# Where a hybrid decoder trunk prepares its weights: low halves moved from GpSimd to VectorE, high halves all on ScalarE, weights loaded in 512 KB pieces

## The chip, the cores and the metric

The kernel runs on one core of one Trainium2 chip. That core has TensorE (PE in the profile, its weight loads PEld), VectorE (DVE), ScalarE (ACT), GpSimd (POOL) and SyncE (SP, which here only issues transfers). Each engine works through its own list of instructions strictly in order. The metric is the device time of one launch in microseconds (us), as the median of several runs.

## The reference, cut to what matters

Four layers, with the token mixers A, B, C, A. Each layer applies a normed mixer and a normed gated feed-forward block, all in float32, on 256 tokens of 1024 features.

```
for i in range(DEPTH):
    y = rms_norm(h, g[0])
    y = dilated_attention(...) | sink_window_attention(...) | nsa_attention(...)
    h = h + rms_norm(y, g[1])
    y = conv_ffn(rms_norm(h, g[2]), w_up, conv_w, conv_b, w_down)
    h = h + rms_norm(y, g[3])
```

A has 16 heads in three dilated groups (its input weights are 1024 x 9216), B has sliding windows with a learned sink logit per head, C has compressed, selected and windowed keys, where the compression is a small product of its own (`w1`, `w2`). The feed-forward block is 1024 to 2 x 2816 and back. All weights together are some 240 MB, each read once.

## The kernel before, in words

**Split numbers.** TensorE multiplies in a format with fewer bits than float32. So every operand is kept as a high and a low half, `src = hi + lo`, and each product is three matmuls: high by high, high by low, low by high (`mm3`, lines 308 to 310). For activations and weights alike, `split` (lines 267 to 273) makes `hi` by a rounding copy (line 272 on ScalarE, or line 270 on VectorE) and `lo` by a subtraction (line 273, on VectorE or GpSimd).

**Weights.** They are packed on the host into units of 128 x 1024 float32 (512 KB), in the order in which they are used. `U` units make one tile `raw`, loaded by one transfer that SyncE issues (`load`, line 277); here `U = 2`, so a tile has 1 MB, and the tag has two buffers. `next_unit` takes the next unit and splits it into `wh` and `wl`, which have six buffers each (`WBUFS`); a few units of each output product lie in a pool of their own. A `raw` buffer is free for the next load when the last subtraction that reads it is done. A `wh`/`wl` buffer is free when TensorE's last matmul with it is done.

**Who splits a unit.** `pool_every` = n sends the low half of every n-th unit to GpSimd; 0 sends none. `vhi` = n sends the high half of every n-th unit to VectorE. Both are set stage by stage from the table `TUNED` on line 47:

```
gp = self.pool_every and u % self.pool_every == 0
vh = self.vhi and u % self.vhi == 0
self.split(hi, lo, self.raw[:, j * UNIT : (j + 1) * UNIT], nc.gpsimd if gp else None, vh)
```

Before the change the entries are: `AEV` 3 and `AQ` 3 (A's heads: every third low half on GpSimd), `AO` 2 (A's output weights: every second), `EVB1` 1 (B from its keys and values on: every one), `EVB4` 1 with `VHB` 1 (B's output weights: low half on GpSimd, high half on VectorE), `EVC4` 1 with `VHC` 3 (C's output weights: low half on GpSimd, every third high half on VectorE), `EVF` 6 (the feed-forward's up product: every sixth low half on GpSimd).

**Stages.** In each of the four layers: a mixer, then the feed-forward block. A mixer begins with `early` (four units, token tile 0 while the norm of tile 1 still runs, then tile 1 once `yT`, the transposed and split input, is there), goes on with the other projections, then works pair of heads by pair of heads: logits `s` (line 815), minimum and exponential (line 489 on VectorE, line 490 on ScalarE), division (line 499 on VectorE, and lines 924 in B and 1123 in C on GpSimd), transposition `pT`, split into `pt`, product `ot` (line 531), `o`, `oT`, and the product `y_o` with the output weights. B needs `nsink`, the negated sinks, 128 x 16 (line 875, on VectorE), for its first minimum. C compresses its keys first (products `hid`), makes `kc` (line 999) and eight copies `vc` of the compressed values (line 1003, all on VectorE), and its logits `lc` on the compressed keys need `kc`. The feed-forward's up product has 22 blocks of two units each, every block followed by a convolution and a gated activation (lines 1165 to 1173, and the split of `act`) on VectorE and ScalarE; the down product has 22 units.

**Order.** A scheduling layer records the program and writes out each engine's list. It decides the order on each engine from its own estimates, so an edit can move instructions that it does not name.

Of the kernel before, what the change touches and what calls it, by code (L numbers as in the profile page):

```python
# [19 lines left out]
P = 128  # L20
D = 1024
# [14 lines left out]
ROW_B, ROW_C, NROW = 1024, 1408, 1792  # a head's biases by distance: A's groups 2, 1 and 0 in 256, 256 and 512, B's and C's in 384  # L36
SCALE = 0.125
UNIT = 1024
U = 2
# [7 lines left out]
TUNED = {'DUPM': 'pool', 'EVC2': '0', 'EVC3': '0', 'CS': 'gg', 'CM': '13', 'BM': '13', 'FREE': '0', 'EVB1': '1', 'EVB4': '1', 'EVC1': '0', 'EVC4': '1', 'EVF': '6', 'BS': 'gv', 'AS': 'vv', 'AEV': '3', 'TAIL': '2', 'CH1': '1', 'CR4': '0', 'CR6': '0', 'BR4': '0', 'BR6': '1', 'XF': '3', 'XA': '2', 'XB': '3', 'XC': '2', 'PFH': '1', 'WARM': '0', 'RG': 'V', 'ORD': '1', 'E1': '3', 'G1': '1', 'X1': '1', 'GATE': 'G', 'CH0': '0', 'CW0': '9', 'CW1': '9', 'PB': '6', 'PTB': '3', 'VHB': '1', 'VHC': '3', 'BPO': '4', 'CPO': '4', 'BLAG': '1', 'CLAG': '1', 'FDB': 'v', 'FDC': 'v', 'FD': 'v', 'FDL': 'v', 'QB': '5', 'VB': '3', 'PA': '6', 'BA': '2', 'AO': '2', 'AQ': '3', 'AV': '0'}  # L47
# [24 lines left out]
# ---------------------------------------------------------------- layout  # L72
def unit_cols(w, cols):
    """w-stationary: 128 columns of w as [p, k block, column]."""
    return w[:, cols].reshape(KB, P, -1).transpose(1, 0, 2).reshape(P, -1)


def tok_units(w):
    """tokens-stationary: 512 columns of w as four units of [p, 2 k blocks, 512]."""
    blocks = w.reshape(KB, P, 512).transpose(1, 0, 2)  # L80
    return [blocks[:, 2 * i : 2 * i + 2].reshape(P, -1) for i in range(4)]


def a_units(w_in, w_o):
    """Mixer A's columns: (group, q/k/v, head, dim)."""
# [27 lines left out]
def pair_cols(r):  # L113
    """Columns of heads r and 8 + r."""
    return np.concatenate([np.arange(r * HD, (r + 1) * HD), np.arange((8 + r) * HD, (9 + r) * HD)])
# [11 lines left out]
def c_units(w_in, w1, w_o):  # L127
    HQ = H * HD
    kv = [slice(HQ + i * P, HQ + (i + 1) * P) for i in range(6)]  # k_c v_c k_s v_s k_w v_w
# [46 lines left out]
def pack_conv(conv_w, conv_b):  # L176
    """[layer, p, (block, gate/val), tap 0..2 and the bias]"""
    both = np.concatenate([conv_w, conv_b[:, None]], 1)  # layer, 4, 2 * D_FF
    return both.reshape(DEPTH, 4, 2, NFF, P).transpose(0, 4, 3, 2, 1).reshape(DEPTH, P, NFF * 8)
# [12 lines left out]
def shape_constants():  # L192
    """Buckets by distance (times 1 / SCALE) for the rows of biases, masks of mixer C."""
    rows = []  # distances and which of them count
# [22 lines left out]
def halves(first, end):  # L217
    """(block, half): block by block, the last two half by half"""
# [4 lines left out]
# ---------------------------------------------------------------- device  # L223
class Trunk:
# [20 lines left out]
    # PSUM: one tile of two banks, six of one  # L245
# [21 lines left out]
    def split(self, hi, lo, src, engine=None, vh=False):  # L267
        """src = hi + lo exactly, each with 12 significant bits."""
# [6 lines left out]
    def load(self, c):  # L275
        raw = self.wpool.tile([P, U * UNIT], F32, tag="raw", bufs=2, name=f"raw{c}")
        self.nc.sync.dma_start(raw, self.ins["weights"][c])
        return raw
# [24 lines left out]
    def mm3(self, out, lhs, rhs, start, stop):  # L303
        """(lh + ll)(rh + rl) without ll * rl."""
# [7 lines left out]
    # ------------------------------------------------------------ setup  # L312
    def setup(self):
# [8 lines left out]
        self.ahead = [self.load(0)]  # L322
        if int(TUNED.get("X1", "1")):
            self.ahead.append(self.load(1))
            nc.sync.dma_start(self.h[1], ins["x"][P:])
        else:
            nc.sync.dma_start(self.h[1], ins["x"][P:])
            self.ahead.append(self.load(1))
# [6 lines left out]
    def bias_setup(self):  # L335
        """Rows of -8 * (bias or mask) by distance, per head and mask, to DRAM."""
# [18 lines left out]
    def toeplitz(self, dst, head, first, *dims):  # L355
        """dst[p, x] = row[first + p + x]; dims: others than these"""
# [5 lines left out]
    # ------------------------------------------------------------ norms  # L362
    def rstd(self, ms, name):
        """(sum of the two halves' mean squares + eps) ** -0.5"""
# [14 lines left out]
    def square(self, ms, i, x, name):  # L379
        """ms[i] = sum(x ** 2) / D"""  # L380
# [3 lines left out]
    def post_norm(self, t, y, g, name):  # L384
        """h += rms_norm(y) * g"""
# [29 lines left out]
    def transpose_in(self, t, z, yT, name):  # L415
        """yT[:, k, t * 128 ...] = z block k, transposed and split."""
# [17 lines left out]
    # ------------------------------------------------------------ products  # L434
    def proj(self, out, yT, unit):
        """out[n, tok] += w unit (128 columns) by y."""
# [4 lines left out]
    def proj_tok(self, toks, out, yT, units, nk=4):  # L441
        """out[tok, n] for 128 tokens: units hold nk k blocks of n columns each."""
# [7 lines left out]
    def early(self, yT, outs, late):  # L450
        """Columns of tok_units, [n, tok] into outs (four [128, 256]); `late` makes the second token tile of yT."""
# [18 lines left out]
    def rows_mm(self, y, xT, unit, half, start, stop):  # L470
        """Half of y[tok, 1024] += x block by 128 rows of w."""
# [3 lines left out]
    # ------------------------------------------------------------ attention pieces  # L475
# [5 lines left out]
    def stats(self, n, name):  # L481
        """Columns for -max and the sums of n softmaxes."""
        return [self.small.tile([P, n], F32, tag=f"{w}{n}", bufs=6, name=f"{w}_{name}") for w in ("nm", "den")]

    def exps(self, p, s, bias, st, c, floor=BIG):
        """p = exp(logit - max), logit = SCALE * s + bias; floor: minus one more logit, or more than any."""
# [16 lines left out]
    def p_transposed(self, parts, name):  # L503
        """The parts' transposes side by side: [:, 0] high, [:, 1] low."""
# [9 lines left out]
    def pv(self, out, v, parts, name, start, stop):  # L514
        """out[:, 0] + out[:, 1] (by p high and low), or out[:, 0] if padded, += [vh | vl]' p; parts: k0 q0, k0 q1, k1 q1"""
# [17 lines left out]
    def fold(self, o, a, ps, name, how):  # L533
        """o[64 a ...] = (vh p_hi + vl p_hi) + vh p_lo"""
# [49 lines left out]
    def out_proj(self, name, more, gains=False):  # L584
        """Products with w_o: a function of token tile, pair and half."""
# [18 lines left out]
    def out_done(self, part, y, done, finish):  # L604
        """The products with w_o from pair `done` on, token tile 0 first."""
# [14 lines left out]
    def stacked(self, ps):  # L620
        """For the heads a of a pair: [:, a, 0] has q high in the head's rows and q low in the other's,
        [:, a, 1] has k high in both, [:, a, 2] k low in the head's rows and zeros."""
# [13 lines left out]
    # ------------------------------------------------------------ mixers  # L636
    def mixer_a(self, yT, L, finish, late):
# [12 lines left out]
        def proj_v(jobs, late=None, then=None):  # L650
            """Values of group g, pairs hp and hp + 1; the tokens of groups 1 and 2 in turns, for all keys of a token
            have its parity."""
# [20 lines left out]
        def attend_s(hp):  # L673
            """Token tile t: tokens 2 p + t. Key tiles: 0, 1 of group 0, then the queries' own of groups 1 and 2."""
# [110 lines left out]
    def proj_pair(self, yT, r, q):  # L785
        """q of pairs r and r + 1"""
# [5 lines left out]
    def q_done(self, q, r, ps):  # L792
        """q[:, r, a]: high in the rows of head a of pair r, low in the other's."""
# [6 lines left out]
    def k_done(self, kd, kl, ps):  # L800
        """kd[:, i, a]: k_i high of head a in both halves; kl[:, i, a]: k_i low in the rows of head a, else zeros."""
# [19 lines left out]
    def ps_s(self, one, name):  # L821
        """Two banks for logits."""
# [8 lines left out]
    def pairs(self, yT, q, attend_s, attend_pv, L, finish, hook=None):  # L831
        """Attention of all pairs, products with w_o behind it; q of the first four pairs is there."""
# [34 lines left out]
    def mixer_b(self, yT, L, finish, late):  # L867
# [7 lines left out]
        nc.vector.tensor_scalar(nsink, sink, -1.0, None, op0=ALU.mult)  # L875
# [16 lines left out]
        v = att.tile([P, 4, P], F32R, name="v")  # (key tile, group), [vh | vl]  # L892
# [48 lines left out]
    def compress(self, att, ps, L, kc, vc, slot):  # L941
        """Compressed keys (columns by group; high in both halves, low in the group's) and values (a copy per slot of 16 rows)."""
# [62 lines left out]
    def mixer_c(self, yT, L, finish, late):  # L1005
# [19 lines left out]
        # selected and window keys and values, gates; the attention's tiles lie below those of the compression  # L1025
# [287 lines left out]
```

## Time and profile before

| | |
|---|---|
| timed runs (us) | 1626.03, 1627.21, 1627.77; median 1627.21 |
| the profiled execution | span 1624.6 us from the first to the last instruction |
| busy, share of the span | PE 95%, DVE 76%, ACT 60%, POOL 23% |
| TensorE's mean granted clock | 0.985 of full speed |
| weights | 237 loads of 1024 KB, 4.9 us from issue to landing (median) |
| low halves `wl` | 376 on VectorE, 97 on GpSimd |
| high halves `wh` | 463 on ScalarE, 10 on VectorE |

Of the profiled execution only its span is shown; it stands 2.6 us under the median of the timed runs, which also hold what lies around the span. How to read the page and its views: busy time is time in which the engine executes, including an instruction that has started and is held up inside. In the timeline each row gives start, duration, engine, line, operation, what is written from what, how many in a row were merged, and in brackets how long the engine had been idle before and what ended that. PEclk 1.00 is TensorE's upper level of 2.4 GHz, 0.50 its lower one of 1.2 GHz.

### The profile page before, as it was taken

The numbers are of one execution on the slowest core, as the hardware profiler recorded it, in microseconds if no ns is written. First come the engines' busy times: TensorE is split into PE (matmuls) and PEld (weight loads), VectorE is DVE, ScalarE is ACT, GpSimd is POOL, SyncE is SP. The second block draws the span as 40 slices with busy tenths as digits, with TensorE's granted clock in tenths as the row PEclk, the third lists the DMA queues.
The fourth block names the chain that finished last, engine by engine and source line by source line (L and its number), as shares of the span: only waits on it lengthen the run. The fifth ranks groups of instructions, "written<-read, shape, count | busy, mean of one in ns | idle before, by whom it ended". The sixth has DMA issues, their size and how long they took to land. (4 is left out here: it accounts for less than half of the span.)

```text
span 1624.6 us, 28567 instructions
## 1 busy us (share of the span) xinstructions
PE 1541.3 (95%) x10968; PEld 1429.8 (88%) x10968; DVE 1235.0 (76%) x2154; ACT 973.1 (60%) x1715; POOL 366.2 (23%) x334
## 2 busy tenths in 40 slices
PE   7999999999997799999985999999999999999998
PEld 6999998799986679998884879998999999889986
DVE  5778897698755978985588869975687879669864
ACT  5566665576544566664465857654566667557642
POOL 1443323111004611100125401100342432211100
PEclk9999999999999899999997999999999999999999
DMA  6655556455454526555562035546465556455543
GB/s 231 208 191 180 188 177 204 135 205 183 158 206 141 169 75 202 200 184 206 172 214 92 20 132 201 192 153 233 164 205 183 190 172 195 142 180 203 202 174 112
DMA packets 69737, 283.21 MB, mean 174 GB/s; under 512 B 7152, under 2 KB 36336, under 8 KB 39264
## 3 DMA queue, kind: packets, MB, share of 16 engines
q1 hardware_dynamic: 67392, 273.37, 50.1%
q0 software_dynamic: 2208, 8.01, 1.4%
q8 instruction: 87, 1.43, 0.4%
q14 instruction: 50, 0.41, 0.1%
HBM read 280.19 MB, written 1.16 MB: 173 GB/s over the span
## 5 line engine op out<-in xcount | busy, mean ns | idle before, releaser
L272 ACT ACTIVATE wh<-raw 128x1024 fp32r<-128x1024 f32 x463 | 480.4, 1056 | 354.5 <-DMA raw<-in_weights_dram 150.8
L273 DVE TENSOR_TENSOR wl<-raw,wh 128x1024 fp32r<-128x1024 f32 x376 | 474.7, 1277 | 169.9 <-ACT wh L272 167.4
L308 PE MATMUL up<-yT,wh 128*128 128x256 f32 x1280 | 359.6, 281 | 4.5 <-ACT wh L272 2.3
L273 POOL TENSOR_TENSOR wl<-raw,wh 128x1024 fp32r<-128x1024 f32 x97 | 235.0, 2428 | 557.1 <-ACT wh L272 495.8
L309 PE MATMUL up<-yT,wh 128*128 128x256 f32 x1280 | 359.1, 281 | 0.0
L310 PE MATMUL up<-yT,wl 128*128 128x256 f32 x1280 | 359.0, 281 | 0.0
L308 PEld LDWEIGHTS up<-yT,wh 128*128 128x128 f32 x1280 | 242.8, 190 | 5.2 <-ACT wh L272 2.5
L310 PEld LDWEIGHTS up<-yT,wl 128*128 128x128 f32 x1280 | 242.6, 190 | 0.0
L309 PEld LDWEIGHTS up<-yT,wh 128*128 128x128 f32 x1280 | 240.3, 188 | 0.2
L309 PE MATMUL qk<-yT,wh 128*128 128x256 f32 x768 | 215.0, 280 | 0.0
L308 PE MATMUL qk<-yT,wh 128*128 128x256 f32 x768 | 214.9, 280 | 0.0
L310 PE MATMUL qk<-yT,wl 128*128 128x256 f32 x768 | 214.9, 280 | 0.0
L1168 DVE SCALAR_TENSOR_TENSOR c<-up,cw,c 128x255 f32<-128x255 f32 (+1 forms) x352 | 164.2, 477 | 15.4 <-ACT c L1165 12.6
L310 PEld LDWEIGHTS qk<-yT,wl 128*128 128x128 f32 x768 | 144.9, 189 | 2.1 <-issue 1.5
L309 PEld LDWEIGHTS qk<-yT,wh 128*128 128x128 f32 x768 | 145.1, 189 | 1.5 <-issue 0.7
L308 PEld LDWEIGHTS qk<-yT,wh 128*128 128x128 f32 x768 | 145.1, 189 | 1.5 <-ACT vt L272 0.7
L309 PE MATMUL y_ff<-wl,act 128*128 128x512 f32 x352 | 138.6, 394 | 0.0
L310 PE MATMUL y_ff<-wh,act 128*128 128x512 f32 x352 | 138.3, 393 | 0.0
L308 PE MATMUL y_ff<-wh,act 128*128 128x512 f32 x352 | 135.2, 395 | 0.0
L308 PE MATMUL v<-wh,yT 128*128 128x256 f32 x400 | 114.0, 286 | 1.9 <-ACT wh L272 1.6
L1165 ACT ACTIVATE c<-up,cw 128x256 f32<-128x256 f32 x176 | 96.7, 552 | 31.8 <-DVE c L1168 31.5
L309 PE MATMUL v<-wl,yT 128*128 128x256 f32 x400 | 113.7, 285 | 0.7 <-DVE wl L273 0.7
(218 smaller groups left out, 2942.4 us busy)
## 6 DMA issues: line engine op xcount, KB each, us to landing
raw<-in_weights_dram SPq DMA_DIRECT2D x237, 1024.0 KB, 4.9
bias<-rows SPq DMA_DIRECT2D x160, 128.0 KB, 3.7
gain<-in_norm_gains_dram POOLq DMA_DIRECT2D x15, 512.0 KB, 5.1
out_dram<-h SPq DMA_DIRECT2D x2, 512.0 KB, 2.6
h<-in_x_dram SPq DMA_DIRECT2D x2, 256.0 KB, 3.0
gain<-in_norm_gains_dram SPq DMA_DIRECT2D x1, 512.0 KB, 6.4
h<-in_x_dram SPq DMA_DIRECT2D x1, 512.0 KB, 12.3
onehot<-in_onehot_dram SPq DMA_DIRECT2D x1, 448.0 KB, 12.8
```

What stands on the lines that cost most here:

```text
L272: self.nc.scalar.activation(hi, src, AF.Copy)
L273: (engine or self.nc.vector).tensor_tensor(lo, src, hi.bitcast(F32), op=ALU.subtract)
L308: mm(out, lh, rh, start=start, stop=False)
L309: mm(out, lh, rl, start=False, stop=False)
L310: return mm(out, ll, rh, start=False, stop=stop)
L1165: nc.scalar.activation(c[:, j], u, AF.Identity, bias=w[3], scale=w[2])
L1168: nc.vector.scalar_tensor_tensor(c[:, j, n:], in0=u[:, : S - n], scalar=w[k], in1=c[:, j, n:], op0=ALU.mult, op1=ALU.add)
```

## The change

1. `U` is 1 in place of 2 and the tag `raw` has four buffers in place of two: 473 loads of 512 KB in place of 237 of 1 MB, in the same 2 MB of buffers. The start loads four such tiles ahead in place of two large ones.
2. `EVB1`, `EVB4`, `EVC4`, `EVF` and `AO` become 0: outside A's heads every low half of a weight is made on VectorE. GpSimd keeps the 40 of A's heads.
3. `VHB` and `VHC` become 0: every high half is made on ScalarE.
4. `nsink` is made on ScalarE.

Comments and docstrings are taken out as well, which changes no instruction.

```diff
-U = 2
+U = 1
...
-        raw = self.wpool.tile([P, U * UNIT], F32, tag="raw", bufs=2, name=f"raw{c}")
+        raw = self.wpool.tile([P, U * UNIT], F32, tag="raw", bufs=4, name=f"raw{c}")
         self.nc.sync.dma_start(raw, self.ins["weights"][c])
...
-        self.ahead = [self.load(0)]
+        self.ahead = [self.load(0), self.load(1)]
         if int(TUNED.get("X1", "1")):
-            self.ahead.append(self.load(1))
+            self.ahead += [self.load(2), self.load(3)]
             nc.sync.dma_start(self.h[1], ins["x"][P:])
...
-        nc.vector.tensor_scalar(nsink, sink, -1.0, None, op0=ALU.mult)
+        nc.scalar.activation(nsink, sink, AF.Copy, scale=-1.0)
```

In the table `TUNED`: `EVB1`, `EVB4`, `EVC4`, `VHB` from 1 to 0, `VHC` from 3 to 0, `EVF` from 6 to 0, `AO` from 2 to 0; the other entries stay.

**VectorE at the entry of B**, from the norm's second token tile to the first minimum. Before (`yT` is the input of the products, `q`, `kl` and `vT` come out of B's projections, `L489` is the first minimum):

```order
L426 TENSOR_TENSOR yT_1_0_5589<-zT_0_1_0_5771,yT_1_0_5588 128x4x128
L875 TENSOR_SCALAR nsink<-sink 128x16
L426 TENSOR_TENSOR yT_1_0_5589<-zT_0_1_1_5778,yT_1_0_5588 128x4x128
L798 TENSOR_TENSOR q<-q_0_5717,q 64x2x256
L798 TENSOR_TENSOR q<-q_1_5718,q 64x2x256
L798 TENSOR_TENSOR q<-q_0_5717,q 64x2x256
L798 TENSOR_TENSOR q<-q_1_5718,q 64x2x256
L809 TENSOR_TENSOR kl<-kv_5827,kd 64x256 x2
L888 COPY vT<-kv_5827 128x256
L489 ISA p_1_0_0_5910,nm_0_5904<-s_0_0_5906,bias_0_0_5908,nsink 128x128
```

Now:

```order
L426 TENSOR_TENSOR yT_1_0_5735<-zT_0_1_0_5921,yT_1_0_5734 128x4x128
L426 TENSOR_TENSOR yT_1_0_5735<-zT_0_1_1_5928,yT_1_0_5734 128x4x128
L273 TENSOR_TENSOR wl_5981<-raw_5978,wh_5980 128x1024
L273 TENSOR_TENSOR wl_6011<-raw_6008,wh_6010 128x1024
L273 TENSOR_TENSOR wl_6097<-raw_6094,wh_6096 128x1024
L273 TENSOR_TENSOR wl_6127<-raw_6124,wh_6126 128x1024
L273 TENSOR_TENSOR wl_6199<-raw_6196,wh_6198 128x1024
L273 TENSOR_TENSOR wl_6229<-raw_6226,wh_6228 128x1024
L798 TENSOR_TENSOR q<-q_0_5863,q 64x2x256
L798 TENSOR_TENSOR q<-q_1_5864,q 64x2x256
L273 TENSOR_TENSOR wl_6470<-raw_6467,wh_6469 128x1024
L273 TENSOR_TENSOR wl_6476<-raw_6473,wh_6475 128x1024
```

`nsink` no longer stands between the two halves of `yT`, and eight of B's fourteen low halves stand on VectorE before its `q` are finished.

**VectorE in C**, from the compressed keys `kc` and values `vc` to the logits of the next pair. Before:

```order
L798 TENSOR_TENSOR q<-q_9446,q 64x2x256
L999 TENSOR_TENSOR kc_8811<-cmp_9333,kc_8810 64x16
L273 TENSOR_TENSOR vhl<-cmp_9336,vhl 128x64
L1003 TENSOR_SCALAR vc<-vhl,cst 128x128 x6
L999 TENSOR_TENSOR kc_8811<-cmp_9333,kc_8810 64x16
L1003 TENSOR_SCALAR vc<-vhl,cst 128x128 x2
L798 TENSOR_TENSOR q<-q_9446,q 64x2x256
L489 ISA p_2_1_0_9574,nm_1_0_9576<-s_1_0_0_9578,bias_1_0_9572 128x128
```

Now:

```order
L999 TENSOR_TENSOR kc_9041<-cmp_9581,kc_9040 64x16
L1111 RECIPROCAL den_0_1_9633<-den_0_1_9633 128x4
L273 TENSOR_TENSOR vhl<-cmp_9584,vhl 128x64
L999 TENSOR_TENSOR kc_9041<-cmp_9581,kc_9040 64x16
L1117 TENSOR_TENSOR rg_0_1_9649<-den_0_1_9633,gate 128x4
L1003 TENSOR_SCALAR vc<-vhl,cst 128x128 x8
L273 TENSOR_TENSOR wl_10260<-raw_10257,wh_10259 128x1024
L798 TENSOR_TENSOR q<-q_9694,q 64x2x256
L273 TENSOR_TENSOR wl_10278<-raw_10275,wh_10277 128x1024
L273 TENSOR_TENSOR wl_10266<-raw_10263,wh_10265 128x1024
L798 TENSOR_TENSOR q<-q_9694,q 64x2x256
L273 TENSOR_TENSOR wl_10284<-raw_10281,wh_10283 128x1024
```

Both parts of `kc` now come ahead of all eight `vc`, and four low halves of the output weights have taken the place behind them; the other four stand a little earlier or later in the same list.

## Rows read from the trace of the kernel before

**Rows 1.** The page, part 1: busy us, share of the span, instructions

```profile
PE 1541.3 (95%) x10968; PEld 1429.8 (88%) x10968; DVE 1235.0 (76%) x2154; ACT 973.1 (60%) x1715; POOL 366.2 (23%) x334
```

**Rows 2.** Windows: length; PE, PEld, DVE, ACT, POOL busy; PEclk; DMA share; GB/s

```profile
320.00:425.00 105.00, 102.70 (x874) 102.53 (x873) 93.45 (x150) 72.38 (x119) 14.38 (x6) 1.00 0.56 192
...
512.00:516.00 4.00, 4.00 (x10) 3.19 (x11) 0.00 (x0) 0.00 (x0) 0.00 (x0) 0.53 0.82 281
520.00:587.00 67.00, 54.16 (x347) 47.32 (x346) 59.50 (x166) 43.65 (x130) 31.23 (x26) 0.92 0.35 103
835.00:880.00 45.00, 27.74 (x185) 23.46 (x184) 37.94 (x74) 25.19 (x62) 26.19 (x16) 0.82 0.49 165
```

**Rows 3.** Groups by line: operation, shapes, count | busy us, mean ns | idle before

```profile
L272 ACT ACTIVATE wh<-raw 128x1024 fp32r<-128x1024 f32 x463 | 480.4, 1056 | 354.5 <-DMA raw<-in_weights_dram 150.8 <-PE up L309 70.7 <-PE qk L309 51.9
L273 DVE TENSOR_TENSOR wl<-raw,wh 128x1024 fp32r<-128x1024 f32 x376 | 474.7, 1277 | 169.9 <-ACT wh L272 167.4 <-issue 1.0
...
L273 POOL TENSOR_TENSOR wl<-raw,wh 128x1024 fp32r<-128x1024 f32 x97 | 235.0, 2428 | 557.1 <-ACT wh L272 495.8 <-PE up L310 26.2 <-PE s L815 17.3
```

**Rows 4.** Timeline at the entry of B, 502 to 513 us: VectorE, GpSimd, TensorE

```profile
502.39 9.54 DVE L875 TENSOR_SCALAR nsink<-sink 128x16 f32<-128x16 f32 x1 [1.21 <-DMA sink<-in_b_sinks_dram]
...
502.61 9.28 POOL L273 TENSOR_TENSOR wl<-raw,wh 128x1024 fp32r<-128x1024 f32 x4
...
512.00 0.80 PE L310 MATMUL early<-wh,yT 128*128 128x512 f32 x1 [7.74 <-DVE yT L426]
```

**Rows 5.** Inside B, 520 to 590 us: VectorE's timeline and groups; TensorE's waits

```profile
541.18 0.15 DVE L915 TENSOR_TENSOR e<-nm,sink 128x4 f32<-128x4 f32 x1
...
L270 DVE CAST wh<-raw 128x1024 fp32r<-128x1024 f32 x8 | 6.7, 874 | 0.0
...
L917 DVE TENSOR_TENSOR den<-den,e 128x4 f32<-128x4 f32 x8 | 5.2, 647 | 0.0
...
PE ot L531 <- DVE pt L273: 5.2, 2, 4.7
...
PE s L815 <- DVE nm L489: 3.8, 2, 3.3
```

**Rows 6.** Inside C, 835 to 880 us: VectorE's and GpSimd's timeline, TensorE's waits

```profile
850.08 10.17 DVE L1003 TENSOR_SCALAR vc<-vhl,cst 128x128 fp32r<-128x128 f32 x6
...
850.71 9.26 POOL L273 TENSOR_TENSOR wl<-raw,wh 128x1024 fp32r<-128x1024 f32 x4
...
PE lc L1060 <- DVE kc L999: 8.5, 1, 8.5
...
PE ot L531 <- DVE pt L273: 4.0, 1, 4.0
```

**Rows 7.** Feed-forward, up product, 339 to 343 us: GpSimd and VectorE

```profile
339.47 2.40 POOL L273 TENSOR_TENSOR wl<-raw,wh 128x1024 fp32r<-128x1024 f32 x1 [12.81 <-ACT wh L272]
...
339.73 2.42 DVE L273 TENSOR_TENSOR act<-g,act 128x256 fp32r<-128x256 f32 x1 [0.30 <-ACT act L272]
...
342.47 0.41 DVE L273 TENSOR_TENSOR act<-g,act 128x256 fp32r<-128x256 f32 x1
```

**Rows 8.** Entry of the feed-forward block: loads; TensorE's waits in layers 0 and 1

```profile
314.48 13.65 SPq L277 DMA_DIRECT2D raw<-in_weights_dram  x4
...
PE up L308 <- ACT wh L272: 2.3, 1, 2.3
...
PE up L308 <- DVE c L1168: 1.8, 1, 1.8
```

**Rows 9.** The page, part 6, DMA issues: count, KB each, median us to landing

```profile
raw<-in_weights_dram SPq DMA_DIRECT2D x237, 1024.0 KB, 4.9
...
gain<-in_norm_gains_dram POOLq DMA_DIRECT2D x15, 512.0 KB, 5.1
```

**Rows 10.** TensorE's timeline at the kernel's start and in C's compression

```profile
12.55 0.58 PE L308 MATMUL v<-wh,yT 128*128 128x256 f32 x1 [1.63 <-ACT wh L272]
...
828.07 0.44 PE L1043 MATMUL gt<-ident,gT 128*128 128x128 f32 x2 [3.29 <-ACT gT L1040]
```

More of the change, by code (lines that the diff above doesn't have):

```diff
@@ L46 @@
 WBUFS = 6
-TUNED = {'DUPM': 'pool', 'EVC2': '0', 'EVC3': '0', 'CS': 'gg', 'CM': '13', 'BM': '13', 'FREE': '0', 'EVB1': '1', 'EVB4': '1', 'EVC1': '0', 'EVC4': '1', 'EVF': '6', 'BS': 'gv', 'AS': 'vv', 'AEV': '3', 'TAIL': '2', 'CH1': '1', 'CR4': '0', 'CR6': '0', 'BR4': '0', 'BR6': '1', 'XF': '3', 'XA': '2', 'XB': '3', 'XC': '2', 'PFH': '1', 'WARM': '0', 'RG': 'V', 'ORD': '1', 'E1': '3', 'G1': '1', 'X1': '1', 'GATE': 'G', 'CH0': '0', 'CW0': '9', 'CW1': '9', 'PB': '6', 'PTB': '3', 'VHB': '1', 'VHC': '3', 'BPO': '4', 'CPO': '4', 'BLAG': '1', 'CLAG': '1', 'FDB': 'v', 'FDC': 'v', 'FD': 'v', 'FDL': 'v', 'QB': '5', 'VB': '3', 'PA': '6', 'BA': '2', 'AO': '2', 'AQ': '3', 'AV': '0'}
+TUNED = {'DUPM': 'pool', 'EVC2': '0', 'EVC3': '0', 'CS': 'gg', 'CM': '13', 'BM': '13', 'FREE': '0', 'EVB1': '0', 'EVB4': '0', 'EVC1': '0', 'EVC4': '0', 'EVF': '0', 'BS': 'gv', 'AS': 'vv', 'AEV': '3', 'TAIL': '2', 'CH1': '1', 'CR4': '0', 'CR6': '0', 'BR4': '0', 'BR6': '1', 'XF': '3', 'XA': '2', 'XB': '3', 'XC': '2', 'PFH': '1', 'WARM': '0', 'RG': 'V', 'ORD': '1', 'E1': '3', 'G1': '1', 'X1': '1', 'GATE': 'G', 'CH0': '0', 'CW0': '9', 'CW1': '9', 'PB': '6', 'PTB': '3', 'VHB': '0', 'VHC': '0', 'BPO': '4', 'CPO': '4', 'BLAG': '1', 'CLAG': '1', 'FDB': 'v', 'FDC': 'v', 'FD': 'v', 'FDL': 'v', 'QB': '5', 'VB': '3', 'PA': '6', 'BA': '2', 'AO': '0', 'AQ': '3', 'AV': '0'}
 XF = int(TUNED.get("XF", "3"))
@@ L327, in setup @@
             nc.sync.dma_start(self.h[1], ins["x"][P:])
-            self.ahead.append(self.load(1))
+            self.ahead += [self.load(2), self.load(3)]
         self.ident = self.const.tile([P, P], F32, name="ident")
```

## The prediction, as it was put on record

> **What bounds the kernel now.** The page's first part comes first: TensorE is busy for 1541.3 of the 1624.6 us [rows 1]. So nothing can be won where TensorE works without a pause, and the question is what the change does to the 83 us in which it does not, and to the stretches in which it runs at its lower clock. The windows say where these are: in the feed-forward's up product TensorE is busy for 102.7 of 105 us at full clock, but in B for 54.2 of 67 us and in C, between 835 and 880 us, for 27.7 of 45 us at 0.82 of full speed [rows 2]. In B and C VectorE is the busiest engine of the window (59.5 and 37.9 us), and GpSimd is busy for 31.2 and 26.2 us [rows 2], mostly with low halves of weights at 2.4 us each [rows 3].
>
> The timelines then show what VectorE is busy with. At B's entry `nsink`, an instruction on 128 x 16 numbers, lasts 9.54 us, and ends when four back-to-back low halves on GpSimd end (502.61 + 9.28 = 511.89 us). The second half of `yT` stands behind it, and TensorE sits idle for 7.74 us until it comes [rows 4]. In C six small copies `vc` last 10.17 us in all, beside four GpSimd low halves of 9.26 us; `kc` stands behind them, and TensorE waits 8.5 us for it [rows 6]. In the up product a split of `act` takes 2.42 us beside a GpSimd low half and 0.41 us without one [rows 7]. I read this as: while GpSimd works on a weight, those VectorE instructions cannot proceed. The low halves that GpSimd takes over therefore do not relieve VectorE; each blocks it for up to 2 us and saves it 1.28 us [rows 3].
>
> **The change part by part.** All terms are changes of the end time.
>
> *B's entry.* No low half runs on GpSimd there any more, and `nsink` has left VectorE's list. The 7.74 us go. When TensorE resumed, it ran at 0.53 of full speed for the 4 us of the window behind [rows 2], with a matmul of 0.80 us [rows 4]; without the pause I expect full speed, which saves 4.0 x 0.47 = 1.9 us. What comes in: eight low halves, 8 x 1.28 = 10.2 us [rows 3], ahead of or among the `q`. They lie beside TensorE's rest of `early` and B's key product, and `q` waits for those anyway; if that cover were 3 to 4 us short, the term would be 6. Take -9.6, ends -6 and -9.6.
>
> *Inside B.* VectorE loses eight high halves (6.7 us) and the stalls: eight small sums L917 at 0.647 us mean, against 0.15 us for an instruction of the same size, are 4.0 us [rows 5]. It gains the six other low halves, 7.7 us. Net -3 us on the busiest engine, more if the stalls of instructions not listed go too. TensorE's waits on VectorE in this stretch are 5.2 + 3.8 = 9.0 us [rows 5]: that is the most that can come back. ScalarE takes eight high halves more, 8.4 us on 43.7 of 67 [rows 2, 3], and does not become the bound. Take -4, ends 0 and -9.
>
> *C's entry into attention.* The wait of 8.5 us for `kc` [rows 6] goes: `kc` now precedes `vc`, and nothing on GpSimd holds either. Take -8.5, lower end -6 if the added low halves push `kc` back.
>
> *Inside C.* VectorE gets eight low halves, 10.2 us, and loses two high halves and the small stalls. It has 45 - 37.9 = 7 us idle in the window [rows 2]. One more wait of TensorE is on VectorE, 4.0 us for `pt` [rows 6]. Take -3, ends 0 and -4.
>
> *Up product of the feed-forward.* In a window of 105 us GpSimd makes six low halves [rows 2]. VectorE takes them, 6 x 1.28 = 7.7 us, and is rid of up to six stalls of 2 us. Even with no stall gone it would be at 93.5 + 7.7 = 101.2 of 105 us, and TensorE has no gap of weight in this stretch. Take 0, upper end +2 over all four blocks.
>
> *A's output weights.* Four low halves per layer go to VectorE, 5.1 us each time, at the end of A's attention. GpSimd's instructions leave the same stretch. Take 0, ends -2 and +4.
>
> *Loads of 512 KB.* SyncE issues 237 more transfers, off the path. What matters is the turn of a buffer: a tile of 1 MB becomes free only after two low halves, and its successor lands 4.9 us after its issue [rows 9]. At the feed-forward's entry the first free tile is issued at 314.48 us, and TensorE then waits 2.3 us for a high half in layer 0, and 1.8 us in layer 1 behind the same train [rows 8]. With units freed one by one the first load starts about one low half earlier, and half the bytes land no later. Take -3 of these 4.1 us, ends 0 and -4.1. In C's compression, where units are used fastest, TensorE waits 3.29 us for `gT` [rows 10], which stands on ScalarE among high halves that wait for loads: take -2, ends 0 and -3.3. At the start the first matmul waits 1.63 us for the first high half [rows 10], and a tile of half the size lands sooner: take -1.5, ends 0 and -1.6.
>
> The nearest row for a 512 KB load is the gain vector's, 5.1 us [rows 9]. It is issued from GpSimd and reads one row 128 times, so I take it as the upper end; the lower is half of 4.9 us, and with four loads in flight either will do, since the up product uses a unit in 105 / 874 x 24 = 2.9 us [rows 2] and a buffer thus has 4 x 2.9 = 11.5 us to turn. The Trainium skill (DMA: Bandwidth & Descriptors, section Bandwidth) speaks against this edit: transfers should be batched to at least 1 MiB for 75% of peak, and from its 0.95 us for 64 KB and 6.15 us for 1 MB an estimate for 512 KB is 3.4 us, about a tenth more per byte. By the rule the three load terms would be nil and the sum smaller by 6.5 us; no run here shows a 512 KB weight load yet.
>
> *Sum:* -9.6 - 4 - 8.5 - 3 - 3 - 2 - 1.5 = -31.6 us on the profiled span of 1624.6, so 1593.0. The median of the timed runs is 2.6 us above that span, so I say **1595.6 us**. The low ends of all terms together give about -6 to -12, the high ends about -42.
>
> **The rivals.**
> *VectorE becomes the bound of B and C.* The big waits go, but the added low halves (14 and 8 of them, 28 us in all) fill the room, TensorE waits elsewhere for `pt` and `nm`, and the inner terms and the load terms vanish: -18 us or less, 1605 to 1614 us. For it: VectorE is at 89% in B's window. Against it: much of that is stall.
> *The stall has another cause.* If `vc` and `yT` were slow for a reason of their own, neither wait goes, VectorE just gets more work, and only the load terms stay: 1621 to 1628 us. Against it: the stalled spans end with GpSimd's instructions, three times at different stages.
> *Half-size loads become the bound (slower).* In the four up products a unit is due every 2.9 us, and four buffers allow 11.5 us from issue until the low half is done. Conversion takes 1.06 + 1.28 us and its queueing a few us; the point is a landing time of about 8 us. At 9.5 us a unit comes every 3.2 us instead of 2.9; on 4 x 40 units that is +48 us, and with -32 elsewhere about 1643 us. For it: twice as many transfers, and loads with others in flight. Against it: the queue moved 281 GB/s for 4 us [rows 2], where the up product needs 192.
>
> **How the numbers follow.** The forecast, with terms between 60% and 130% of the sum, has a chance of 0.68 (1583 to 1605 us); VectorE as the bound 0.21; another cause 0.05; the loads 0.06. The range 1582 to 1613 holds the first case and nearly all of the second, and leaves out some 0.15. A measurement of this kernel tells about 0.2%, 3.3 us, from no change. Faster by more than that: the first two cases and a bit of the third, 0.91. The rest of the third and a little of the fourth are the same, 0.04; the loads are slower, 0.05.
>
> **What would show it.** Right: in B no VectorE instruction of 9 us, the gap of TensorE before `early` gone and the clock at 1.00 behind it; in C no wait of `lc` for `kc`; B's window some 13 us shorter, C's some 11; the up products as long as before, with GpSimd idle and VectorE at 93 us of 105 again; the entry gaps of the feed-forward at 1 us or less. Wrong: `vc` or `yT` long although GpSimd is idle, TensorE's waits for `pt` grown by what the others lost, or high halves that wait for loads all along the up product.

## The result, and the profile after

The changed kernel takes 1601.3 us in the median of four runs (1598.85 to 1604.7), the kernel before, timed beside it, 1626.62 (1621.66 to 1627.77): a ratio of 0.9854, 95% interval 0.9822 to 0.9886. The forecast was 1595.6 with a range from 1582 to 1613, so sign and range held, and the gain was 25.3 us instead of 31.6. The profiled execution has a span of 1597.1 us, 27.5 less than before.

Part 1 of the page after (busy us, share of the span, instructions; before: [rows 1]):

```profile
PE 1532.3 (96%) x10968; PEld 1421.8 (89%) x10968; DVE 1225.7 (77%) x2200; ACT 982.3 (62%) x1726; POOL 230.9 (14%) x277
```

VectorE has 57 low halves more and is busy for 9 us less. Part 5 after (groups by line, as in [rows 3]) tells why:

```profile
L272 ACT ACTIVATE wh<-raw 128x1024 fp32r<-128x1024 f32 x473 | 495.1, 1058 | 374.6 <-PE up L309 123.7
L273 DVE TENSOR_TENSOR wl<-raw,wh 128x1024 fp32r<-128x1024 f32 x433 | 531.2, 1238 | 159.4 <-ACT wh L272 150.3
...
L273 POOL TENSOR_TENSOR wl<-raw,wh 128x1024 fp32r<-128x1024 f32 x40 | 96.9, 2422 | 170.8 <-ACT wh L272 144.9
```

Part 6 after has the loads, as in [rows 9]:

```profile
raw<-in_weights_dram SPq DMA_DIRECT2D x473, 512.0 KB, 4.4
```

A low half costs 1238 ns in the mean instead of 1277, and the other stalled instructions are short again. Half the bytes land 0.5 us sooner than 1 MB did, between the forecast's bounds (2.45 and 5.1).

The windows after show the up product's GpSimd idle, B and C shifted 10 and 18 us earlier (columns as in [rows 2]):

```profile
320.00:425.00 105.00, 104.23 (x887) 104.06 (x887) 92.95 (x157) 71.54 (x118) 0.00 (x0) 1.00 0.62 194
510.00:577.00 67.00, 52.74 (x339) 46.72 (x339) 56.35 (x168) 50.34 (x138) 6.97 (x16) 0.92 0.45 126
817.00:862.00 45.00, 34.58 (x227) 29.45 (x224) 34.06 (x92) 30.42 (x75) 8.46 (x10) 0.87 0.61 191
```

At B's entry the second half of `yT` stood behind `nsink` before, with the wait of [rows 4]:

```profile
502.47 9.45 DVE L426 TENSOR_TENSOR yT<-zT,yT 128x512 fp32r<-128x512 f32 x1
```

After, from the timeline of all engines, it takes 0.69 us:

```profile
500.34 0.69 DVE L426 TENSOR_TENSOR yT<-zT,yT 128x512 fp32r<-128x512 f32 x1 [0.18 <-ACT yT L425]
...
501.29 4.63 DVE L273 TENSOR_TENSOR wl<-raw,wh 128x1024 fp32r<-128x1024 f32 x4 [0.26 <-ACT wh L272]
...
502.10 0.20 ACT L875 ACTIVATE nsink<-sink 128x16 f32<-128x16 f32 x1
```

But other waits of TensorE came. Its waits after (us in total, times, longest), 515 to 577 us in B, then 815 to 862 us in C; they answer to [rows 5, 6] (`kd` is the high half of B's keys, `nm` the minima of line 489, `pt` the split, transposed attention weights):

```profile
PE s L815 <- ACT kd L806: 5.4, 1, 5.4
PE s L815 <- DVE nm L489: 2.7, 4, 1.0
PE ot L531 <- DVE pt L273: 2.3, 2, 1.8
PE q L308 <- DVE nm L489: 1.9, 1, 1.9
```

```profile
PE lc L1059 <- DVE q L798: 2.0, 2, 1.2
PE s L815 <- DVE nm L489: 1.8, 2, 1.3
PE cmp L992 <- ACT hidT L978: 1.3, 1, 1.3
PE s L815 <- DVE q L798: 1.1, 1, 1.1
```

The wait of 8.5 us for `kc` is gone, and many of about 1 us stand in its place. The 5.4 us in B are new: every profile below in which B's halves are moved has 5.1 to 6.0 us of this wait, and the three without (`nsink` alone, loads alone, loads and `nsink`) have none. ScalarE's timeline has `kd` behind four high halves and two `q`, the first of the halves having waited 4.13 us for its load:

```profile
510.36 1.06 ACT L272 ACTIVATE wh<-raw 128x1024 fp32r<-128x1024 f32 x1 [4.13 <-DMA raw<-in_weights_dram]
...
515.44 0.37 ACT L806 ACTIVATE kd<-kv 64x256 fp32r<-64x256 f32 x1
```

**Two cadences.** One difference belongs to none of this. These windows show the up product's matmuls alone, in the four feed-forward blocks (length; PE, PEld, DVE, ACT; PEclk; DMA share; GB/s), of the changed kernel:

```profile
340.00:390.00 50.00, 50.00 (x427) 50.00 (x426) 17.77 (x38) 10.33 (x19) 1.00 0.62 192
640.00:690.00 50.00, 50.00 (x444) 50.00 (x443) 17.38 (x37) 10.27 (x19) 1.00 0.63 196
1000.00:1050.00 50.00, 50.00 (x443) 50.00 (x442) 17.99 (x38) 9.84 (x18) 1.00 0.65 193
1450.00:1500.00 50.00, 50.00 (x427) 50.00 (x426) 17.16 (x36) 9.86 (x18) 1.00 0.61 186
```

TensorE never pauses in any of them and its clock is granted in full, but 427 or 444 matmuls start in 50 us. From start to start a 128x256 matmul takes 117.8 ns in blocks 1 and 4 and 113.3 ns in blocks 2 and 3; in the trace of before all four are slow. A 128x512 matmul shows 233.3 or 228.9 ns: the surplus is about 4.45 ns per matmul, whatever its width. So I also work with a **net span**: the span less the sum of what each start-to-start interval behind a 256-column matmul of 115.5 to 121 ns (231 to 237 behind one of 512 columns) has over 113.3 (228.9). For before that is 1624.6 - 28.9 = 1595.7 us, for the changed kernel 1597.1 - 19.8 = 1577.3. So the cadence accounts for 9.1 us between the two profiles, and 18.4 are left for the edits and for whatever else differs between two executions.

### The profile page after: what moved, and what is told of

Same layout as the page of the kernel before. It is cut to its first block, busy times and chain, and to the rows that moved or that the text cites. A ratio compares the mean times of both kernels' runs of the same rounds, so it can differ in the third digit from the quotient of the medians.

```text
span 1597.1 us, 29233 instructions
## 1 busy us (share of the span) xinstructions
PE 1532.3 (96%) x10968; PEld 1421.8 (89%) x10968; DVE 1225.7 (77%) x2200; ACT 982.3 (62%) x1726; POOL 230.9 (14%) x277
## 5 line engine op out<-in xcount | busy, mean ns | idle before, releaser
L272 ACT ACTIVATE wh<-raw 128x1024 fp32r<-128x1024 f32 x473 | 495.1, 1058 | 374.6 <-PE up L309 123.7
L273 DVE TENSOR_TENSOR wl<-raw,wh 128x1024 fp32r<-128x1024 f32 x433 | 531.2, 1238 | 159.4 <-ACT wh L272 150.3
L1168 DVE SCALAR_TENSOR_TENSOR c<-up,cw,c 128x255 f32<-128x255 f32 (+1 forms) x352 | 164.3, 477 | 9.0 <-ACT c L1165 6.1
L369 POOL TENSOR_TENSOR r_post<-v_post,neg_half 128x1 f32<-128x1 f32 x16 | 8.9, 554 | 789.4 <-DVE v_post L367 789.4
L273 POOL TENSOR_TENSOR wl<-raw,wh 128x1024 fp32r<-128x1024 f32 x40 | 96.9, 2422 | 170.8 <-ACT wh L272 144.9
```

The source lines that it names most:

```text
L272: self.nc.scalar.activation(hi, src, AF.Copy)
L273: (engine or self.nc.vector).tensor_tensor(lo, src, hi.bitcast(F32), op=ALU.subtract)
L369: self.p_last = nc.gpsimd.tensor_tensor(r, v, self.neg_half, op=ALU.pow)
L1168: nc.vector.scalar_tensor_tensor(c[:, j, n:], in0=u[:, : S - n], scalar=w[k], in1=c[:, j, n:], op0=ALU.mult, op1=ALU.add)
```

## The experiments

All figures of stages come from the profile of each run. A stage ends where the first `z_post` (L391) behind it starts, so it takes in the beginning of the next norm; net means less the slow cadence's surplus. Net stages in us; A1 and A4 are the two A layers, F1 to F4 the feed-forward blocks, and "end" is what follows the last `z_post`. The medians in the last column were not all timed together: beside them the kernel before took 1626.6 us (first row and "changed"), 1619.1 ("again", loads alone, halves and `nsink`), 1622.8 (`nsink` alone) and 1625.1 (loads and `nsink`), so times are compared by the ratios below, each to the kernel before timed beside it.

| kernel | A1 | F1 | B | F2 | C | F3 | A4 | F4 | end | net span | median of runs |
|---|---|---|---|---|---|---|---|---|---|---|---|
| before | 283.0 | 188.3 | 105.0 | 185.5 | 164.3 | 186.7 | 277.7 | 187.0 | 18.3 | 1595.7 | 1626.6 |
| changed | 284.6 | 185.4 | 96.4 | 184.0 | 158.9 | 185.2 | 279.1 | 184.5 | 19.4 | 1577.3 | 1601.3 |
| changed, again | 285.5 | 184.4 | 97.1 | 184.0 | 158.9 | 185.7 | 277.9 | 184.5 | 19.4 | 1577.5 | 1599.9 |
| loads alone | 286.9 | 184.8 | 104.4 | 183.3 | 159.6 | 185.6 | 279.3 | 184.3 | 19.4 | 1587.6 | 1599.4 |
| halves and `nsink` alone | 286.7 | 186.1 | 96.3 | 183.6 | 157.5 | 184.9 | 277.6 | 187.6 | 18.3 | 1578.6 | 1598.2 |
| `nsink` alone | 283.8 | 189.0 | 96.2 | 185.3 | 164.3 | 186.7 | 279.8 | 188.1 | 18.3 | 1591.5 | 1609.0 |
| loads and `nsink` | 284.8 | 185.3 | 97.5 | 183.3 | 158.0 | 186.0 | 278.3 | 184.2 | 19.4 | 1576.8 | 1594.8 |

Two profiles of the changed kernel agree within 0.2 us net, although one drew the slow cadence in blocks 1 and 4 and the other in 3 and 4. That agreement is better than the measure is: two profiles of another program ("added pauses" below) differ by 2.9 us net, 2.7 of it in B, so a difference of this size between single profiles does not show an effect by itself. A1 is the least steady stage (281.8 to 288.9 over all profiles). Without it the net spans fall into clear groups: 1312.7 us before, 1307.7 for `nsink` alone, 1300.7 for the loads alone, and 1291.9 to 1292.7 for the changed kernel (twice), halves and `nsink`, and loads and `nsink`.

**The changed kernel again.** 

> The changed kernel once more, for the scatter and for the matmul cadence in a second profile. 1599 to 1605 us. If the cadence belongs to the program, the same two of the four up products (blocks 2 and 3) run at 113.3 ns; if it is a matter of the execution, others do.

1599.86 us, ratio 0.9889 (0.9859 to 0.9920): 19.2 us less than the kernel before timed beside it, where the first four runs had shown 25.3. The same windows as above, now of this execution:

```profile
340.00:390.00 50.00, 50.00 (x443) 50.00 (x443) 18.74 (x40) 10.99 (x20) 1.00 0.66 200
640.00:690.00 50.00, 50.00 (x443) 50.00 (x442) 17.72 (x38) 9.87 (x18) 1.00 0.67 194
1000.00:1050.00 50.00, 50.00 (x427) 50.00 (x426) 16.59 (x36) 9.88 (x18) 1.00 0.62 189
1450.00:1500.00 50.00, 50.00 (x427) 50.00 (x426) 17.17 (x36) 9.91 (x18) 1.00 0.63 185
```

Block 1 is now the fast one and block 3 slow: the cadence is drawn per execution, not by the program.

**Loads alone.** `U = 1`, four `raw` buffers and the four first loads; the table of options and `nsink` as before.

> The kernel before with 512 KB loads and four buffers alone; GpSimd keeps all its low halves, VectorE its high halves and nsink. Theory (GpSimd's weights hold VectorE): both long waits of TensorE (7.7 us at B's entry, 8.5 us in C) stay, only the load terms come: 4 to 7 us less than before, 1620 to 1623 us. Rival (the loads make the gain): 20 us less or more, 1600 to 1607 us. Cadence of the up product's matmuls (113.3 or 117.8 ns): if the loads set it, blocks 2 and 3 are fast here as in the changed kernel and the time is 9 us lower still.

1599.42 us, ratio 0.9887 (0.9865 to 0.9909): by the time alone, the rival, for the changed kernel's repeat beside it had 0.9889. By the trace, neither as put. At B's entry nothing has changed (VectorE's timeline):

```profile
498.36 9.57 DVE L875 TENSOR_SCALAR nsink<-sink 128x16 f32<-128x16 f32 x1 [1.19 <-DMA sink<-in_b_sinks_dram]
498.45 9.49 DVE L426 TENSOR_TENSOR yT<-zT,yT 128x512 fp32r<-128x512 f32 x1
```

In C, however, the wait of 8.5 us for `kc` is gone though all of GpSimd's low halves are still there. Before, the second `kc` stood behind six of the `vc` (VectorE's timeline):

```profile
860.28 0.18 DVE L999 TENSOR_TENSOR kc<-cmp,kc 64x16 fp32r<-64x16 f32 x1
```

With the loads alone the order and the times are others (VectorE's timeline, then GpSimd's):

```profile
838.93 0.16 DVE L999 TENSOR_TENSOR kc<-cmp,kc 64x16 fp32r<-64x16 f32 x1
...
839.34 0.18 DVE L999 TENSOR_TENSOR kc<-cmp,kc 64x16 fp32r<-64x16 f32 x1
839.55 5.79 DVE L1003 TENSOR_SCALAR vc<-vhl,cst 128x128 fp32r<-128x128 f32 x8
```

```profile
842.09 2.39 POOL L273 TENSOR_TENSOR wl<-raw,wh 128x1024 fp32r<-128x1024 f32 x1
846.56 10.01 POOL L273 TENSOR_TENSOR wl<-raw,wh 128x1024 fp32r<-128x1024 f32 x4 [2.08 <-ACT wh L272]
```

Both `kc` stand ahead of `vc`, and the train of four meets no `vc` (compare [rows 6]). These are two changes at once, of the order and of the times, and no run has the new order with the train still on the `vc`; with `kc` ahead, the `vc` can no longer hold it up, whatever GpSimd does. The eight `vc` are in fact still held, by other instructions of GpSimd: 5.79 us, against 1.66 without any (below). The loads are worth 9.5 us in the feed-forward blocks and 4.7 in C. The time is short beyond that because all four up products of this profile drew the fast cadence (a surplus of 11.4 us in all, before 28.9). Yet two of the other three executions were 2.7 and 3.4 us shorter than this one, so the cadence is not all of the scatter.

**Halves and `nsink` alone.** The options and `nsink` of the change; `U = 2` and two buffers.

> The kernel before with the moved halves and nsink on ScalarE alone; loads stay at 1 MB with two buffers. Theory (GpSimd's weights hold VectorE): both long waits go, VectorE has no instruction of 9 us, and most of the gain is here: 18 to 22 us less than before, 1604 to 1609 us. Rival (the stall has another cause): 1622 to 1632 us, with the waits at their places. Cadence: if GpSimd's absence from the up product sets it, at least two of the four blocks run at 113.3 ns.

1598.21 us, ratio 0.9875 (0.9835 to 0.9916), net 17.1 us less than before: both waits went, B gave 8.7 and C 6.8 us. In C the order is the old one here, with the second `kc` behind the `vc`, but no GpSimd instruction lies beside them (VectorE's timeline):

```profile
834.91 1.66 DVE L1003 TENSOR_SCALAR vc<-vhl,cst 128x128 fp32r<-128x128 f32 x8
836.60 0.18 DVE L999 TENSOR_TENSOR kc<-cmp,kc 64x16 fp32r<-64x16 f32 x1
```

So the `vc` were held by GpSimd, and taking its train away is enough. The parts do not add: 8.1 and 17.1 us apart, 18.4 together, since either cures C.

**`nsink` alone.**

```diff
-        nc.vector.tensor_scalar(nsink, sink, -1.0, None, op0=ALU.mult)
+        nc.scalar.activation(nsink, sink, AF.Copy, scale=-1.0)
```

> The kernel before with nsink alone moved to ScalarE; GpSimd keeps its four low halves in a row at B's entry. Theory as predicted (GpSimd's weights hold yT too): yT's second half still takes 9 us, TensorE's wait of 7.7 us ahead of early stays, B's stage 105 to 106 us. Rival (only nsink is held, and yT stands behind it): yT takes 0.7 us, the wait is under 1 us, B's stage 96 to 98 us, so this one line is all of B's gain.

1609.03 us, ratio 0.9914 (0.9881 to 0.9947). That is the rival: TensorE's wait of 7.7 us is gone and B's net stage falls from 105.0 to 96.2 us, all that the whole change gains in B, with the four low halves of GpSimd still in place. Timeline of VectorE and GpSimd:

```profile
498.33 0.69 DVE L426 TENSOR_TENSOR yT<-zT,yT 128x512 fp32r<-128x512 f32 x1 [0.18 <-ACT yT L425]
...
499.59 9.49 POOL L273 TENSOR_TENSOR wl<-raw,wh 128x1024 fp32r<-128x1024 f32 x4
...
507.38 2.64 DVE L798 TENSOR_TENSOR q<-q,q 64x512 fp32r<-64x512 f32 x4 [8.36 <-ACT q L797]
...
519.31 1.29 DVE L915 TENSOR_TENSOR e<-nm,sink 128x4 f32<-128x4 f32 x1
```

`yT` is over before the train here; but `q`, of the same kind (a PSUM tile less an SBUF tile), runs 2.64 / 4 = 0.66 us beside it, undisturbed. (`e` in the last row has two SBUF inputs and takes 1.29 us beside another low half, against 0.15 in [rows 5].) So `yT` was never held by GpSimd: it stood behind `nsink`, which was. Sorting the VectorE instructions of the trace of before that start inside a GpSimd low half of a weight with over 0.7 us of it left gives the same line: those that read PSUM keep their time (`c<-up,cw,c` 24 of 24 at 0.47 to 0.48 us, `pt<-pT,pt` 12 at 0.56 to 0.69), those with two SBUF inputs do not (14 `act` with a median of 1.98 instead of 0.42, 15 `wl` with 2.58 instead of 1.22). The Trainium skill (SBUF — State Buffer, Who interferes with whom) states this rule: an instruction of VectorE with at most one SBUF input, outside the modes that use both ports, does not contend with GpSimd, while one with two SBUF inputs, and `tensor_scalar` in such a mode, do. The trace agrees, and by that rule I could have priced `yT` at nothing beforehand.

**`nsink` back on VectorE**, all else changed.

> The changed kernel with nsink back on VectorE. Both theories that name GpSimd: nsink takes 0.2 us there, B's stage 97 to 98 us as in the changed kernel, time 1595 to 1605 us. Rival (nsink is slow for a reason of its own, such as its load): it lasts over 5 us, and B's stage is 104 us or more.

1599.66 us, ratio 0.9844 (0.9811 to 0.9878), net 1577.2, B 97.6 net. VectorE's timeline:

```profile
500.77 0.26 DVE L875 TENSOR_SCALAR nsink<-sink 128x16 f32<-128x16 f32 x1 [1.18 <-DMA sink<-in_b_sinks_dram]
```

Without a train beside it, `nsink` is harmless: it needs the two together, and taking away either is enough.

**Loads and `nsink`.** The two edits above, no half moved.

> The kernel before with two edits of the change alone: 512 KB loads with four buffers, and nsink on ScalarE; every low and high half stays where it was. Net span here means the span less what the slow matmul cadence adds (before 1595.7, changed kernel 1577.3 and 1577.5, loads alone 1587.6 us). Theory now (nsink is B's gain, the loads are C's, the moved halves are worth nothing beside them): net span 1577 to 1581 us. Forecast (the moved halves carry the inner terms of B and C and C's entry, 10 us or more): net span 1587 us or more.

1594.78 us, ratio 0.9817 (0.9779 to 0.9855), net 1576.8: these two edits give the whole gain. Moving 57 low halves off GpSimd and 10 high halves off VectorE gives nothing beside them that these profiles can tell. The same holds for the other pairs: halves and `nsink` reach 1578.6 us net, loads and halves (the run before this one) 1577.2. So any two of the three parts give the whole gain, and the third adds nothing that can be seen.

**C's halves put back** (`EVC4` 1, `VHC` 3) in the changed kernel.

> The changed kernel with C's halves back where they were (low halves on GpSimd, every third high half on VectorE). Theory as predicted (the split makes C's gain): C's stage 5 us longer than in the changed kernel (160.2), 165 us. Rival (the loads alone keep GpSimd's train away from vc; the loads-only run had 160.9): 159 to 161.5 us, C's edits worth 1 us or less beside the loads.

1600.89 us, ratio 0.9862 (0.9826 to 0.9897); C's stage is 160.9 (159.6 net against 158.9). The rival: beside the loads, C's edits are worth 0.7 us, within the scatter.

**Every sixth low half of the feed-forward put back** (`EVF` 6).

> The changed kernel with every sixth low half of the feed-forward back on GpSimd. Forecast's term for the up product (nothing): the same time as the changed kernel within 2 us, 1599 to 1604 us. If the 113.3 ns cadence of blocks 2 and 3 comes from GpSimd being idle there, they fall back to 117.8 ns, and the time rises by 8 to 9 us, to about 1610 us.

1595.49 us, ratio 0.9867 (0.9835 to 0.9900), net 1574.1. Not slower; the four blocks take 1.5 us less net, and the span 3.2, which is about what two profiles of one program differ by. The pause of TensorE after 64 to 68 matmuls of the up product, for VectorE's `c` or a high half (0.1 to 0.9 us in the changed kernel's four blocks), is left in one block of four. In the runs with small loads and `EVF` 6 it is left in one block each; in those with `EVF` 0 or 1 MB loads in three or four.

**No low half on GpSimd in A's heads either** (`AEV` and `AQ` 0).

> The changed kernel with no low half on GpSimd at all: those of A's heads go to VectorE too. There p and oT are still held by GpSimd, 11 us in each of the two A layers. If VectorE has room in A (185 of 220 us busy, TensorE 219.5 of 220): no difference, A's first stage 288 to 290 us, the fourth layer's 282 to 283 us. If its 40 more low halves at 1.24 us bind: up to 10 us slower. A gain is not expected, since TensorE does not wait in A's heads.

1594.53 us, ratio 0.9818 (0.9762 to 0.9873), net 1571.7. If it is a gain, one that I did not expect: 2.0 and 2.4 us net in the two A stages, 1.6 in B and C together (against the changed kernel's first profile). Between 50 and 270 us VectorE is busy for 194.28 us instead of 185.18, but TensorE for all 220.00 instead of 219.54. That is only 0.5 us of it; where the rest comes from stays open, and the times (1588.48 to 1603.62) overlap those of the changed kernel.

**Both of these.**

> The changed kernel with A's heads without low halves on GpSimd, and with every sixth low half of the feed-forward back on it. If the two effects seen apart add (net span 5.7 us and 3.3 us shorter than the changed kernel's 1577.4): net span 1567 to 1570 us, time 1585 to 1592 us by cadence. If they are the same few us of A's stage: net span 1571 to 1574 us.

1592.1 us, ratio 0.9816 (0.9767 to 0.9865), net 1569.7: they nearly add (5.6 + 3.2 of 8.8 came as 7.6). This is the shortest net span, 7.6 us ahead of the changed kernel's, but the times alone (1591.16 to 1604.08) overlap, and loads and `nsink`, timed beside it, have the same ratio.

**No low halves of output weights in B and C.**

```diff
+            if self.nolo:
+                nc.scalar.activation(hi, self.raw[:, j * UNIT : (j + 1) * UNIT], AF.Copy)
+                return hi, hi
```

> The changed kernel without the low halves of the eight units of output weights in B and in C: they are left out, and the high half stands in their place in the products, so TensorE and ScalarE have the same work and VectorE 10 us less in each stage. If VectorE's own busy time is what binds B and C now (the first rival): B's stage (97.2) and C's (160.2) each 5 to 10 us shorter. If TensorE's short waits there are chains of single instructions: each within 1.5 us of the changed kernel.

The high half stands in for the missing low one in these products. 1596.73 us, ratio 0.9818 (0.9760 to 0.9876); B's stage 94.8 (97.2 and 97.9 with them), C's 156.3 (160.2). Neither case as put: some 10 us less work for VectorE gives 2.4 to 4.0 us in C (seven profiles with C's low halves on VectorE have 158.7 to 160.3). For B nothing follows, since the run with added pauses, which has all its low halves, shows 94.9 us too. Windows of this run, where VectorE was busy for 56.35 and 34.06 us above:

```profile
510.00:577.00 67.00, 54.26 (x367) 47.84 (x366) 47.78 (x159) 50.02 (x138) 6.68 (x16) 0.95 0.48 147
817.00:862.00 45.00, 37.83 (x245) 31.72 (x243) 26.58 (x90) 31.35 (x79) 8.05 (x10) 0.84 0.62 200
```

So VectorE's work is a part of what bounds C, not the bound, and in B no part is shown; the rest, by TensorE's waits, is chains of single instructions.

**Added pauses.**

```diff
+                        if i in (9, 15) and j == 0:
+                            ctx.enter_context(self.tc.issue_after(done.ins))
                         self.proj(ps[:, j * S : (j + 1) * S], yT, unit)
```

> The run with every sixth low half of the feed-forward on GpSimd, and in each of the four up products two more pauses of TensorE: at blocks 9 and 15 the first matmul waits for the activation of the block before (some 3 us each, 25 us in all). Theory (a pause in TensorE's stream draws anew which of the two matmul cadences follows, 113.3 or 117.8 ns, and nothing else changes it): every change of cadence inside an up product lies at a pause, and some of the eight added ones change it. Rival (the cadence follows the clock time or the load on the chip): changes lie anywhere, and the cadence is the same on both sides of the added pauses.

This one failed: no start-to-start interval over 150 ns appears at blocks 9 and 15, so TensorE was not held and the run (1595.57 us, ratio 0.9820, two timed runs) is a repeat of its base (`EVF` 6), with the same instructions in the same order on every engine. As a repeat it tells how far single profiles go. B's stage in the base, then here (length; PE, PEld, DVE, ACT, POOL; PEclk; DMA share; GB/s):

```profile
477.17:574.86 97.69, 83.08 (x496) 72.27 (x495) 75.05 (x195) 66.03 (x167) 11.81 (x30) 0.93 0.45 130
472.38:567.26 94.88, 80.36 (x496) 69.53 (x495) 75.10 (x194) 65.88 (x167) 11.89 (x30) 0.96 0.47 134
```

The same program takes 2.8 us less in B at a granted clock of 0.96 instead of 0.93, and its net span is 1571.2 us against 1574.1. The net span takes out the cadence, not the clock. What the run was to show can in part be read from the natural pauses. In all fourteen profiles (before, changed and the twelve runs) I cut the up products where two matmuls start more than 125 ns apart. Every piece of 64 to 932 matmuls is either fast throughout (means 113.34 to 113.48) or slow throughout (117.77 to 117.79); none is mixed. The cadence changes only at a pause, and behind the one after 64 to 68 matmuls it is slow in 24 of 40 cases, ahead of it in 2; a slow piece behind it costs 862 x 4.45 ns = 3.8 us more than a fast one. In the up products without that pause the long piece is slow in 5 of 16. So slow pieces are more frequent behind that pause, but that the pause brings them on is not shown, as no pause was added on purpose.

## Why the prediction was right, and where its terms were off

By net stages of the two profiles:

| term of the sum | forecast | measured net |
|---|---|---|
| start; A's output weights (A1) | -1.5 | +1.6 (again: +2.5) |
| B's entry and inside B | -9.6 - 4 | -8.6 (-7.9) |
| C: compression, entry, inside | -2 - 8.5 - 3 | -5.4 (-5.4) |
| feed-forward entries | -3 | -8.4 (-8.9) |
| A4 and the end | 0 | +2.5 (+1.3) |
| sum (net spans) | -31.6 | -18.4 (-18.2) |
| cadence | not thought of | -9.1 (-8.4) |

*B's entry: right place, wrong reason in part.* The wait of 7.7 us went. The forecast had GpSimd hold `nsink` and `yT`; the `nsink` run shows that it held `nsink` alone. Of the 9.6, the 1.9 for the clock did not come: the added halves made `kd` late, TensorE paused for 5.4 us, and the granted clock stood at 0.5 from 515.9 to 522.8 us. The forecast had named this cover as 3 to 4 us short at worst.

*Inside B and inside C: nil instead of -4 and -3.* Loads and `nsink` without any moved half reach 97.5 us in B and 158.0 in C, the changed kernel 96.4 to 97.1 and 158.9, no difference beyond the scatter. The stalls of [rows 5, 6] went but for two `vc` (0.64 and 1.08 us), yet in C the low halves that VectorE took on cost about what that freed; the run without them shows their price, 2.4 to 4.0 us. To that extent the first rival (VectorE fills its room) was right. In B the price is not known.

*C's entry: the wait of 8.5 us went, the stage gave 5.4.* The step that failed is "the wait is the gain": `lc` and `s` now wait for `q` and `nm` in many small pieces, for which the one long wait had left time. And the cause was not the split alone: the loads by themselves put `kc` ahead of `vc`, moved GpSimd's train away from `vc` and gave 4.7. In the compression the wait for `gT` fell from 3.3 us to 2.2, where the forecast had taken 2 us.

*Loads: too small by a factor of three.* The forecast took 3 of the 4.1 us of waits in two entries. Loads alone give 3.5, 2.2, 1.1 and 2.7 us in the four blocks. The two waits that it had named went whole: TensorE's waits in blocks 1 and 2 fall from 3.4 and 2.7 us to 1.1 and 0.9. The other 5.4 us lie where it had looked for nothing, about half of them in the down products; their cause stays open. At the start nothing came: the wait of 1.6 us for the first high half [rows 10] went, but TensorE paused for 0.9 us for a low half behind it, and A1 as a whole did not shorten. The Trainium skill's rule of at least 1 MiB per transfer (DMA: Bandwidth & Descriptors, Bandwidth) did not decide here: 4.4 us for 512 KB (the estimate from its table was 3.4) is more per byte than 4.9 for 1 MB, and the loads gained all the same. Size and number of buffers were changed together, so which of the two gained is not shown.

*Up product: 0 was nearly right by its own work* (1.5 us net over four blocks for the opposite edit), but the forecast did not know that the cadence of the 862 matmuls behind a pause there can be another.

*A4 and the end.* The end takes 18.3 us in the three profiles with 1 MB loads and 19.4 in all those with 512 KB, a cost of the loads that the forecast did not have; its cause stays open. A4 (277.9 and 279.1 against 277.7) is within the scatter.

*Slips in the working.* SyncE issues 236 transfers more, not 237; 60% to 130% of the sum is 1586 to 1608 us, not 1583 to 1605; and "-18 us or less" for the first rival begins at 1609 us, not 1605. None of them moves the forecast.

So the sign and the two long waits were right by their mechanism, but that the total came so near is luck: 13 us too much from the edits were made good by 9 us between these two profiles that no step of the working held. Repeated, the same kernel gained 19.2 us.

## What to carry to other kernels

Before work is moved off GpSimd because it holds VectorE, find the instruction that is held, by its operands: here it was one of 16 columns, and one line for it gave all of B's gain. A wait's length is not the gain of its removal: 8.5 us in C gave 5.4, and 7.7 us at B's entry gave 8.8 with `nsink` alone. Edits that cure the same collision do not add, so run each part alone. And before a difference below one per cent is put down to an edit, compare the start-to-start times of like matmuls in stretches without a pause, and the granted clock stage by stage.

## What the runs showed of the hardware

In these traces the up product's stream of weight loads and matmuls runs at one of two spacings, 113.3 or 117.8 ns for 256 columns, at the same granted clock of 1.00, and keeps it until TensorE pauses. The surplus is 11.4 to 28.9 us in the profiles here. Some 10 us of it lie outside the feed-forward blocks and hardly change; the up products hold 0.4 to 15.9, as much as the 17 us by which all the runs of the kernel before scatter (1614 to 1631 us), though only one of these was profiled. What sets the spacing behind a pause stays open.

Second, the 0.2 us `nsink` started 0.2 us ahead of the first of four GpSimd low halves in a row and still ended only with the last [rows 4]. But GpSimd had been at work already when `nsink` started at 502.39 us, filling `kl` until 502.63 (GpSimd's timeline):

```profile
501.96 0.67 POOL L808 MEMSET kl<- 64x256 f32 x2
502.61 2.39 POOL L273 TENSOR_TENSOR wl<-raw,wh 128x1024 fp32r<-128x1024 f32 x1
```

So the row had no gap, and `nsink` was not let through between two of its instructions. In C it was otherwise: the `vc` beside the four low halves ended one by one, each 0.1 us behind one of them (VectorE, then GpSimd):

```profile
850.75 2.40 DVE L1003 TENSOR_SCALAR vc<-vhl,cst 128x128 fp32r<-128x128 f32 x1
850.71 2.36 POOL L273 TENSOR_TENSOR wl<-raw,wh 128x1024 fp32r<-128x1024 f32 x1
```

What decides between the two stays open.
